# Top-2 dispatch on one core: the first store moved behind the first loads, both groups' first stores issued later

## The chip, the core and the metric

The kernel runs on one core of a Trainium2 chip. The metric is the device time of one execution in microseconds (us); of several executions the median is given. The profile comes from one further execution, taken by the hardware profiler; its times are counted from the start of its span.

## What is computed

For each of 16 x 1024 = 16384 tokens there are 512 float32 values `x` and 8 router logits. The softmax over the logits, the two highest probabilities and their renormalising give two weights per token; the output holds, for each token, its `x` row times the lower weight and its `x` row times the higher one:

```python
topk_probs = topk_probs / np.sum(topk_probs, axis=-1, keepdims=True)
x_expanded = x[:, :, np.newaxis, :].repeat(k, axis=2)
return (x_expanded * topk_probs[..., np.newaxis]).astype(np.float32)
```

The softmax's own sum falls out in the renormalising, so the two weights are the sigmoid of the difference of the two highest logits, with either sign. 33.6 MB of `x` and 0.5 MB of logits are read and 67.1 MB of output are written; each output row is one product.

## The kernel before, in words

**Tiling.** The 16384 tokens lie on 128 partitions with 128 tokens ("rows" below) each. They are worked on in two groups of 65 and 63 rows per partition (`GROUPS`, L42). One input row is 2 KB per partition, one output row, both products, 4 KB. The tile `xs` (L95) holds one group's input rows; the tile `osp` (L96) has room for 18 output rows. Output rows go either to `osp` or back into `xs`, over input rows that are no longer needed (L111 to 115).

**Loads.** A group's input comes in three loads (`LOADS`, L44): 6, 28 and 31 rows in the first group, 4, 28 and 31 in the second. They are issued on SyncE's queue (SP, L139), but the second group's first load goes out on ScalarE's (ACT) queue, behind a small copy (L128) that waits until the first group's fourth store has landed. Behind the first load come the two loads of the logits (L144, L145), for both groups at once.

**Weights.** `top2_weights` (L14 to 38) finds the two highest logits of each token on VectorE (DVE) with max and min, in room borrowed from `osp`, and gets both weights on ACT by two sigmoids, into `WA`.

**Products and stores.** `STORES` (L47 to 50) lists each store as (first row, rows, tile, place): in the first group 3, 15, 16, 15 and 16 rows, alternately from `osp` and `xs`, the first two both from `osp`; in the second 16, 16, 15 and 16. For each entry DVE multiplies the rows by their weights in one instruction (L164) or in two (`cuts`, L152): where `osp` is used again, the first `FREE[g]` rows go ahead, since their place comes free earlier. Of the second group's first entry the last `ACT_ROWS` = 4 rows are multiplied by ACT instead, two instructions a row (L157). Behind the products the entry's store is issued (L176): on SP, but the very first one, of three rows, on ACT.

**Order.** `keep_in_program_order` keeps the loads and stores of a queue in the order of the text. An engine that issues a DMA waits first for what the DMA needs: a store for its products, a load of the second group for the stores that read the rows it overwrites. On the DMA engines the packets of one queue go out in order; a packet of these transfers is one partition's whole contiguous piece, up to 64 KB. So SP's order in the first group is: load 6, logits twice, load 28, load 31, store 15, store 16, store 15, store 16, then the second group's loads of 28 and 31 and its four stores.

Of the kernel before, what the change touches and what calls it, by code (L numbers as in the profile page):

```python
# [1 line left out]

# [4 lines left out]

F32 = mybir.dt.float32
ALU = mybir.AluOpType
ACTF = mybir.ActivationFunctionType  # L10
P = 128


def top2_weights(nc, WA, dlt, room, logits, E):  # L14

    tt = nc.vector.tensor_tensor
    hi, lo, n = None, None, E  # L20
    while n > 1:
        n //= 2
        if hi is None:
            a, b = logits[:, :, 0:n], logits[:, :, n : 2 * n]
            nhi, nlo = room(n), b
            tt(nhi, a, b, op=ALU.max)  # L26
            tt(nlo, a, b, op=ALU.min)  # L27
        else:
            a, b = hi[:, :, 0:n], hi[:, :, n : 2 * n]
            nhi, nlo, tmp = room(n), room(n), room(n)  # L30
            tt(tmp, lo[:, :, 0:n], lo[:, :, n : 2 * n], op=ALU.max)  # L31
            tt(nlo, a, b, op=ALU.min)  # L32
            tt(nlo, nlo, tmp, op=ALU.max)  # L33
            tt(nhi, a, b, op=ALU.max)  # L34
        hi, lo = nhi, nlo
    tt(dlt, hi[:, :, 0], lo[:, :, 0], op=ALU.subtract)  # L36
    nc.scalar.activation(WA[:, :, 0], dlt, ACTF.Sigmoid, scale=-1.0)  # L37
    nc.scalar.activation(WA[:, :, 1], dlt, ACTF.Sigmoid, scale=1.0)  # L38

GROUPS = [65, 63]  # L42

LOADS = [[6, 28, 31], [4, 28, 31]]  # L44
BASE = [0, 1]

STORES = [  # L47
    [(0, 3, "osp", 0), (3, 15, "osp", 3), (18, 16, "xs", 0), (34, 15, "osp", 0), (49, 16, "xs", 33)],
    [(0, 16, "osp", 2), (16, 16, "xs", 0), (32, 15, "osp", 0), (47, 16, "xs", 32)],
]  # L50

L = 18

FREE = [3, 2]

ACT_ROWS = 4


@with_exitstack
def kernel(  # L60
    ctx: ExitStack,
    tc: tile.TileContext,
    x: bass.AP,
    router_logits: bass.AP,
    k: bass.AP,
    out: bass.AP,
):
    nc = tc.nc
    B, S, D = x.shape
    E = router_logits.shape[-1]  # L70
    N = B * S
    assert int(k) == 2 and E == 8 and N == P * sum(GROUPS)
    M = N // P

    x_v, o_v, rl_v = [], [], []
    t0 = 0
    for n in GROUPS:
        t1 = t0 + P * n
        x_v.append(
            x.rearrange("b s d -> (b s) d")[t0:t1].rearrange("(p m) d -> p m d", p=P)  # L80
        )
        o_v.append(
            out.rearrange("b s k d -> (b s) k d")[t0:t1].rearrange(
                "(p m) k d -> p m k d", p=P
            )
        )
        rl_v.append(
            router_logits.rearrange("b s e -> (b s) e")[t0:t1].rearrange(
                "(p m) e -> p m e", p=P
            )  # L90
        )
        t0 = t1

    wpool = ctx.enter_context(tc.tile_pool(name="wpool", bufs=1))
    xs = wpool.tile([P, max(GROUPS), D], F32)  # L95
    osp = wpool.tile([P, L, 2, D], F32)  # L96
    WA = wpool.tile([P, M, 2], F32)
    dlt = wpool.tile([P, M], F32)


    flat = osp.rearrange("p l k d -> p (l k d)")
    taken = [0]

    def room(n):
        o = taken[0]
        taken[0] += M * n
        return flat[:, o : o + M * n].rearrange("p (m n) -> p m n", n=n)

    logits = room(E)

    def place(where, at, n):  # L111

        if where == "osp":
            return osp[:, at : at + n]
        return xs[:, at : at + 2 * n, :].rearrange("p (r k) d -> p r k d", k=2)

    m0 = 0
    stores = []
    for g, G in enumerate(GROUPS):
        x0, r = BASE[g], 0  # L120
        for n in LOADS[g]:

            late = g == 1 and r == 0
            if late:


                rows = xs[:, x0 : x0 + 2, :]
                pause = nc.scalar.activation(rows, rows, ACTF.Copy)  # L128
                tc.add_manual_dep(
                    pause.ins,  # L130
                    stores[-2].ins.name,
                    mybir.DependencyInfo(
                        mybir.DependencyClass.Sync, mybir.DependencyReason.DATA
                    ),
                    reason="begin when the store ahead of the last has landed",
                )
                tc.keep_in_program_order(pause)
            queue = nc.scalar if late else nc.sync
            load = queue.dma_start(xs[:, x0 + r : x0 + r + n, :], x_v[g][:, r : r + n, :])  # L139
            tc.keep_in_program_order(load)  # L140
            r += n
            if g == 0 and r == 6:
                n0 = GROUPS[0]
                tc.keep_in_program_order(nc.sync.dma_start(logits[:, :n0], rl_v[0]))  # L144
                tc.keep_in_program_order(nc.sync.dma_start(logits[:, n0:], rl_v[1]))  # L145
                top2_weights(nc, WA, dlt, room, logits, E)
        assert r == G
        for r, n, where, at in STORES[g]:
            og = place(where, at, n)

            again = where == "osp" and at == 0 and r > 0
            cuts = [0, FREE[g], n] if again else [0, n]  # L152
            if g == 1 and r == 0:
                cuts = [0, n - ACT_ROWS]
                for j in range(n - ACT_ROWS, n):
                    for k2 in range(2):
                        nc.scalar.activation(  # L157
                            og[:, j, k2, :],
                            xs[:, x0 + r + j, :],
                            ACTF.Copy,  # L160
                            scale=WA[:, m0 + r + j, k2 : k2 + 1],
                        )
            for a, b in zip(cuts, cuts[1:]):
                nc.vector.tensor_tensor(  # L164
                    og[:, a:b],
                    xs[:, x0 + r + a : x0 + r + b, :]
                    .unsqueeze(2)
                    .to_broadcast([P, b - a, 2, D]),
                    WA[:, m0 + r + a : m0 + r + b, :]
                    .unsqueeze(3)  # L170
                    .to_broadcast([P, b - a, 2, D]),
                    op=ALU.mult,
                )

            queue = nc.scalar if g == r == 0 else nc.sync
            stores.append(queue.dma_start(o_v[g][:, r : r + n], og))  # L176
            tc.keep_in_program_order(stores[-1])
        m0 += G


# [1 line left out]
_INS = ['x', 'router_logits', 'k']  # L182
_OUTS = [((16, 1024, 2, 512), 'float32')]

_NUMBERS = {'k': 2}


# [26 lines left out]
```

## Time and profile before

| | |
|---|---|
| median of 3 runs | 240.56 us (239.94 to 240.78) |
| span of the profiled execution | 238.1 us |
| DVE, ACT busy in it | 137.6 us, 7.9 us |
| read, written | 34.08 MB, 67.11 MB |
| mean rate over the span | 425 GB/s |
| DMA packets | 2448 |

Of the profiled execution the span alone is known, from its first instruction to its last; the launch and what closes the execution lie outside it. The median of the runs, which are taken without the profiler, is 2.5 us above this span. Busy time of an engine is the time in which it carries out instructions; issuing a DMA and waiting do not count. The DMA engines, sixteen of them, have a row of their own in the 40 slices and shares by queue: q1 is the queue that SP issues to, q10 the one of ACT.

### The profile page before, as it was taken

To read this page: it belongs to the slowest core of one execution; us is meant where nothing else is said; L and a number is where in the kernel's file an instruction comes from. 1 tells how busy PE (TensorE), PEld (TensorE's weight loads), DVE (VectorE), ACT (ScalarE), POOL (GpSimd) and SP (SyncE) were. 2 spreads that over 40 slices of the span, in tenths; PEclk is the share of its full clock that TensorE was granted. 3 is DMA by queue.
4 is the path that set the end of the run, shared out by engine and by line. 5 is a ranking of instruction groups with operands and counts; after the bars stand their busy time and mean duration, and the time that the engine had idled before them with its cause. 6 is when DMAs were issued, how large, how long until landed. Compare 5 with 4: busy or idle time off the path is not lost.

```text
span 238.1 us, 115 instructions
## 1 busy us (share of the span) xinstructions
DVE 137.6 (58%) x22; ACT 7.9 (3%) x12; POOL 0.2 (0%) x4
## 2 busy tenths in 40 slices
DVE  0560499999789999100000009999936999950000
ACT  2000000000000000010000007000000000000000
POOL 0000000000000000000000000000000000000000
DMA  7979998979998999989999899898989989979894
GB/s 262 533 337 519 430 418 374 496 341 495 462 396 374 506 433 392 495 352 483 486 396 417 376 479 501 352 506 363 517 363 451 429 363 495 485 341 517 352 528 176
DMA packets 2448, 101.19 MB, mean 425 GB/s; under 512 B 272, under 2 KB 400, under 8 KB 528
## 3 DMA queue, kind: packets, MB, share of 16 engines
q1 hardware_dynamic: 2160, 98.57, 96.1%
q10 hardware_dynamic: 288, 2.62, 2.6%
HBM read 34.08 MB, written 67.11 MB: 425 GB/s over the span
## 4 chain that ended last, share of the span: by engine, by line
DMA 50%; DVE 38%; SPq 1%; issue 0%; DVEq 0%
DMA xs<-in_x_dram 30%; DVE osp L164 24%; DMA out_dram<-osp 20%; DVE xs L164 14%; SPq L144 0%; SPq L145 0%; SPq L139 0%; SPq L176 0%; DVEq L164 0%
## 5 line engine op out<-in xcount | busy, mean ns | idle before, releaser
L164 DVE TENSOR_TENSOR osp<-xs,WA 128x3072 f32<-128x3072 f32 (+4 forms) x7 | 65.1, 9298 | 65.6 <-DMA xs<-in_x_dram 56.8
L164 DVE TENSOR_TENSOR xs<-xs,WA 128x16384 f32<-128x16384 f32 x4 | 68.9, 17225 | 0.2
L157 ACT ACTIVATE osp<-xs,WA 128x512 f32<-128x512 f32 x8 | 5.0, 708 | 37.6 <-DMA xs<-in_x_dram 37.6
L26 DVE TENSOR_TENSOR osp<-osp 128x512 f32<-128x512 f32 x1 | 0.7, 692 | 8.4 <-DMA osp<-in_router_logits_dram 8.4
L128 ACT ACTIVATE xs<-xs 128x1024 f32<-128x1024 f32 x1 | 1.1, 1056 | 90.8 <-DMA out_dram<-osp 90.8
L37 ACT ACT_TABLE_LOAD x1 | 1.3, 1283 | 0.7 <-PEq L195 0.7
L27 DVE TENSOR_TENSOR osp<-osp 128x512 f32<-128x512 f32 x1 | 0.7, 691 | 0.0
L32 DVE TENSOR_TENSOR osp<-osp 128x256 f32<-128x256 f32 (+1 forms) x2 | 0.7, 350 | 0.0
L31 DVE TENSOR_TENSOR osp<-osp 128x256 f32<-128x256 f32 (+1 forms) x2 | 0.7, 350 | 0.0
L33 DVE TENSOR_TENSOR osp<-osp 128x256 f32<-128x256 f32 (+1 forms) x2 | 0.7, 350 | 0.0
L34 DVE TENSOR_TENSOR osp<-osp 128x256 f32<-128x256 f32 (+1 forms) x2 | 0.7, 348 | 0.0
L37 ACT ACTIVATE WA<-dlt 128x128 f32<-128x128 f32 x1 | 0.3, 317 | 10.3 <-DVE dlt L36 10.3
L36 DVE TENSOR_TENSOR dlt<-osp 128x128 f32<-128x128 f32 x1 | 0.3, 292 | 0.0
L38 ACT ACTIVATE WA<-dlt 128x128 f32<-128x128 f32 x1 | 0.3, 299 | 0.0
L195 POOL MEMSET const-bfloat16-1.0<- 128x1 bf16 x1 | 0.1, 102 | 0.0
L195 POOL MEMSET const-uint8-127<- 128x1 uint8 x1 | 0.1, 102 | 0.0
L195 POOL MEMSET const-float32-1.0<- 128x1 f32 x1 | 0.1, 99 | 0.0
L195 POOL MEMSET const-float32-0.0<- 128x1 f32 x1 | 0.1, 98 | 0.2 <-issue 0.2
## 6 DMA issues: line engine op xcount, KB each, us to landing
out_dram<-osp SPq DMA_DIRECT2D x3, 7680.0 KB, 23.4
xs<-in_x_dram SPq DMA_DIRECT2D x2, 7936.0 KB, 40.9
xs<-in_x_dram SPq DMA_DIRECT2D x2, 7168.0 KB, 35.2
xs<-in_x_dram SPq DMA_DIRECT2D x1, 1536.0 KB, 6.2
out_dram<-osp ACTq DMA_DIRECT2D x1, 1536.0 KB, 24.7
xs<-in_x_dram ACTq DMA_DIRECT2D x1, 1024.0 KB, 24.8
osp<-in_router_logits_dram SPq DMA_DIRECT2D x1, 260.0 KB, 6.4
osp<-in_router_logits_dram SPq DMA_DIRECT2D x1, 252.0 KB, 6.6
```

Of the source, the lines that this page charges most:

```text
L26: tt(nhi, a, b, op=ALU.max)
L27: tt(nlo, a, b, op=ALU.min)
L31: tt(tmp, lo[:, :, 0:n], lo[:, :, n : 2 * n], op=ALU.max)
L32: tt(nlo, a, b, op=ALU.min)
L33: tt(nlo, nlo, tmp, op=ALU.max)
L34: tt(nhi, a, b, op=ALU.max)
L36: tt(dlt, hi[:, :, 0], lo[:, :, 0], op=ALU.subtract)
L37: nc.scalar.activation(WA[:, :, 0], dlt, ACTF.Sigmoid, scale=-1.0)
L128: pause = nc.scalar.activation(rows, rows, ACTF.Copy)
L157: nc.scalar.activation(og[:, j, k2, :], xs[:, x0 + r + j, :], ACTF.Copy, scale=WA[:, m0 + r + j, k2 : k2 + 1],)
L164: nc.vector.tensor_tensor(og[:, a:b], xs[:, x0 + r + a : x0 + r + b, :] .unsqueeze(2) .to_broadcast([P, b - a, 2, D]), WA[:, m0 + r + a : ...
L195: nc = _bacc.Bacc("TRN2", target_bir_lowering=False, num_devices=1)
```

## The change

Three things change, all around the first stores of the two groups.

- The first group's first entry (3 rows) no longer gets its store at once on ACT's queue. It is held, and issued on SP directly ahead of the second entry's store (15 rows), with an added dependency on the last product of that second entry, so that both stores are issued together.
- The product of that second entry is cut into one row and fourteen (`cuts = [0, 1, n]`). The one row is of the first load of six; the fourteen are of the load of 28.
- `ACT_ROWS` goes from 4 to 2: of the second group's first entry, DVE multiplies 14 rows instead of 12, and ACT 2 instead of 4. The store of that entry is one store of 16 rows as before.

On the engines' own lists this is: SP has one store more, DVE one instruction more, ACT a DMA and four activations fewer. Bytes and number of DMAs are the same.

```diff
-ACT_ROWS = 4
+ACT_ROWS = 2
...
-    stores = []
+    stores, held = [], []
...
+            if g == 0 and r == 3:
+                cuts = [0, 1, n]
...
-                nc.vector.tensor_tensor(
+                product = nc.vector.tensor_tensor(
...
-            queue = nc.scalar if g == r == 0 else nc.sync
-            stores.append(queue.dma_start(o_v[g][:, r : r + n], og))
-            tc.keep_in_program_order(stores[-1])
+            held.append((r, n, og))
+            if g == r == 0:
+                continue
+            for r2, n2, og2 in held:
+                stores.append(nc.sync.dma_start(o_v[g][:, r2 : r2 + n2], og2))
+                if r2 < r:
+                    tc.add_manual_dep(
+                        stores[-1].ins,
+                        product.ins.name,
+                        mybir.DependencyInfo(
+                            mybir.DependencyClass.Sync, mybir.DependencyReason.DATA
+                        ),
+                        reason="begin with the store behind it",
+                    )
+                tc.keep_in_program_order(stores[-1])
+            held = []
```

## The prediction

> **What bounds the kernel now.** I read the page first: how much of the span do the DMA engines carry packets, and on which queue?
>
> ```profile
> span 238.1 us, 115 instructions
> ...
> DVE 137.6 (58%) x22; ACT 7.9 (3%) x12; POOL 0.2 (0%) x4
> ...
> DMA  7979998979998999989999899898989989979894
> ...
> q1 hardware_dynamic: 2160, 98.57, 96.1%
> q10 hardware_dynamic: 288, 2.62, 2.6%
> ```
>
> The two queues' packets take 96.1 + 2.6 = 98.7% of sixteen engines' span: 0.987 x 238.1 = 235.0 us. DVE, the busiest engine, has 58%. So the chain of waits has to be read with care:
>
> ```profile
> 2.11 24.91 DMA xs<-in_x_dram
> ...
> 27.04 16.17 DVE osp L164
> ...
> 43.23 22.90 DMA out_dram<-osp
> ...
> 66.15 12.97 DVE osp L164
> ```
>
> It puts 38% of the span on DVE, but while DVE multiplies from 27.04 to 43.21 the DMA engines are moving other rows. A DVE step costs time only where the DMA queue runs empty. The busy time by stretches tells whether it ever does. Its last two columns are the DMA share (packet time of the packets that start in the stretch, so it can pass 1) and GB/s; their quotient is the speed while a packet runs.
>
> ```profile
> core 0: us, DVE busy (x) ACT busy (x) POOL busy (x), PEclk, DMA share, GB/s
> 1.60:1.70 0.10, 0.00 (x0) 0.10 (x1) 0.00 (x0) 1.00 0.00 0
> 1.70:5.90 4.20, 0.00 (x0) 0.31 (x1) 0.00 (x0) 1.00 1.01 366
> 17.70:20.50 2.80, 0.00 (x0) 0.00 (x0) 0.00 (x0) 1.00 0.96 394
> 20.50:23.10 2.60, 0.00 (x0) 0.00 (x0) 0.00 (x0) 1.00 1.00 429
> 23.10:26.40 3.30, 0.00 (x0) 0.00 (x0) 0.00 (x0) 1.00 1.01 386
> 26.40:38.50 12.10, 11.46 (x1) 0.00 (x0) 0.00 (x0) 1.00 1.13 489
> 44.80:47.10 2.30, 2.30 (x1) 0.00 (x0) 0.00 (x0) 1.00 1.02 442
> 47.10:157.50 110.40, 61.85 (x6) 6.07 (x9) 0.00 (x0) 1.00 1.00 435
> 157.50:160.00 2.50, 2.50 (x1) 0.00 (x0) 0.00 (x0) 1.00 1.00 406
> 160.00:216.90 56.90, 46.09 (x4) 0.00 (x0) 0.00 (x0) 1.00 1.00 433
> 236.00:238.00 2.00, 0.00 (x0) 0.00 (x0) 0.00 (x0) 1.00 0.00 0
> ```
>
> The first packet starts between 1.60 and 1.80, none starts after 236.0, and the share is 1.00 over the 110.4 us and the 56.9 us between. There is **no idle DMA time to win**. The speed is 434 GB/s in both long stretches, through loads, stores and the change from one to the other. It is lower in three places: the start (366/1.01 = 362), which the change leaves as it is, 17.7 to 26.4, and 157.5 to 160.0 (406). So a change that moves the same bytes can gain only slow packets, and can lose by letting the queue run empty. I looked for both.
>
> **What the slow packets cost.** At 434 GB/s the bytes of the three rows from 17.7 to 26.4 would need 394 x 2.8/434 = 2.54, 429 x 2.6/434 = 2.57 and 386 x 3.3/434 = 2.94 us; their packets took 0.96 x 2.8 = 2.69, 2.60 and 3.33. Lost: 0.15 + 0.03 + 0.40 = 0.58 us; with the rounding of share and rate, 0.5 to 0.65. From 157.5 to 160.0: 2.50 less 406 x 2.5/434 = 2.34, so 0.16 us. From 44.8 to 47.1: 1.02 x 2.3 less 442 x 2.3/434, which is nothing.
>
> What happens there stands in the timeline:
>
> ```profile
> 12.84 3.36 DVE L164 TENSOR_TENSOR osp<-xs,WA 128x3072 f32<-128x3072 f32 x1 [0.58 <-ACT WA L38]
> 16.23 0.38 ACTq L176 DMA_DIRECT2D out_dram<-osp  x1
> 27.04 16.16 DVE L164 TENSOR_TENSOR osp<-xs,WA 128x15360 f32<-128x15360 f32 x1 [10.85 <-DMA xs<-in_x_dram]
> 43.23 0.35 SPq L176 DMA_DIRECT2D out_dram<-osp  x1
> ...
> 60.48 0.34 SPq L176 DMA_DIRECT2D out_dram<-xs  x1
> ...
> 142.37 12.96 DVE L164 TENSOR_TENSOR osp<-xs,WA 128x12288 f32<-128x12288 f32 x1 [46.00 <-DMA xs<-in_x_dram]
> 155.40 0.34 SPq L176 DMA_DIRECT2D out_dram<-osp  x1
> ...
> 172.67 0.34 SPq L176 DMA_DIRECT2D out_dram<-xs  x1
> ```
>
> The early store is issued on ACT's queue at 16.23, and the packets of the 28-row load that start from 17.7 on are slow until 26.4, when that load's packets are out. The store's packets go on beside the next load from 26.4 to 38.5 at 489/1.13 = 433, at full speed. So taking turns costs nothing in itself; the store's first 10 us beside a load do. The 157.5 place also lies about 2 us behind a store's issue (155.40), before the last load's end.
>
> **The change part by part.** *The three-row store leaves ACT's queue for SP's.* Its cost is its packets' time wherever they stand, so it moves and saves nothing by itself. For how long the packets take, and how many stood ahead of the load's end (queue rows of three windows: 16 to 41, 16 to 23.2, 16 to 20.1):
>
> ```profile
> q10 hardware_dynamic: 144, 1.57, 14.8%
> ```
> ```profile
> q10 hardware_dynamic: 31, 0.38, 12.4%
> ```
> ```profile
> q1 hardware_dynamic: 22, 1.26, 74.4%
> ```
>
> All of it is 0.148 x 25 = 3.7 us on each engine, 0.46 for each of an engine's eight packets; 31 packets, two for each of 16 engines, started before the load's last packet. Without them and without the slow packets the 28-row load lands at 27.02 - 0.92 - 0.58 = 25.5, and both loads are through, where the queue now goes over to the store, at 47.1 - 3.7 - 0.6 = 42.8.
>
> *DVE's product of fifteen rows is cut to one and fourteen.* The durations:
>
> ```profile
> L164 DVE TENSOR_TENSOR osp<-xs,WA 128x12288 f32<-128x12288 f32 x2 | 25.9, 12957 | 48.4 <-DMA xs<-in_x_dram 46.0 <-DMA out_dram<-osp 2.4
> L164 DVE TENSOR_TENSOR osp<-xs,WA 128x15360 f32<-128x15360 f32 x1 | 16.2, 16158 | 10.8 <-DMA xs<-in_x_dram 10.8
> ...
> L157 ACT ACTIVATE osp<-xs,WA 128x512 f32<-128x512 f32 x8 | 5.0, 708 | 37.6 <-DMA xs<-in_x_dram 37.6
> ```
>
> A row is (16.158 - 12.957)/3 = 1.07 us, so fourteen take 15.09. The one row belongs to the first six loaded and runs at 16.2, under the 10.85 us in which DVE waited; without that cover it would put 1.1 us on the store's issue. Fourteen rows from 25.5 end at **40.6**. Both stores are issued then, 0.4 us apart by the 0.35 that one takes, while the loads run to 42.8: **2.2 us ahead**, where today 43.23 stands 3.9 ahead of 47.1. The second store is covered by the 3.7 us of the first.
>
> *What stands behind them.* DVE's next product (17.2 us by 43.23 to 60.48) ends at 57.9 instead of 60.4, its store is needed when the two stores are out, 3.7 us and 18.1 us (15 rows' 7.86 MB at 434) after 42.8, at 64.6: more room than now. The three-row product at 57.9 needs the early store landed, by then some 10 us past. From 66.15 on the queue holds the same bytes in the same order, all 0.6 us earlier. SP waited for DVE there anyway, so nothing is queued behind the added wait, and ACT's next instruction waits for the fourth store, as before.
>
> *Second group: two rows go from ACT to DVE.* ACT loses 4 x 0.708 = 2.8 us, beside idle time. DVE's twelve rows become fourteen, 12.96 to 15.09: from 141.8 to 156.9, against a change of queue at 160.2 - 0.6 = 159.6, **2.7 us ahead** (now 4.8). The next store is ready at 156.9 + 17.2 = 174.1 and needed 19.3 us (the 16 rows' 8.39 MB at 434) after 159.6, at 178.9. Hidden.
>
> **How late may a store be issued?** That decides whether 2.2 and 2.7 us are enough, and no row shows it for a queue about to run dry. Bounds:
>
> ```profile
> 0.73 0.38 SPq L139 DMA_DIRECT2D xs<-in_x_dram  x1
> ```
>
> On idle DMA engines: issued at 0.73, first packet from 1.70: 1.0 us. From above: the early store, issued at 16.23, had no packet until 20.1 (the third queue row above has q1 alone), 3.9 us, but two load packets' turns lie in that. At 1.0 us there is no gap. At 3.9 the gaps are 1.7 and 1.2, 2.9 us. I take the 1.0: in the case at hand the queue has nothing left to take a turn, which is like the idle row. The Trainium skill, "DMA: Bandwidth & Descriptors", section "Latency and other measured facts", gives about 600 ns to the first byte for a queue of SP or ACT; by that estimate too both stores come in time, so it leaves the sum as it is.
>
> *New slow packets* beside the later issue: 0 by the 44.8 row, 0.16 us by the 157.5 row. For the first group I take its own row, 0; for the second the 0.16 stays. **Sum: -0.58 us**, out of 238.1. The 240.56 us median of the runs (239.94 to 240.78) lies 2.5 above the profiled span; I keep that difference. 240.56 - 0.58 = **240.0**.
>
> **The rivals.** *A, forecast:* the slow packets were the early store's and go, 240.0 (-0.24%). For it: they begin 1.5 us behind its issue. Against: 26.4 to 38.5 mixes the same two kinds at full speed. *B, more goes:* the 157.5 row's 0.16 too, since that store now comes as the last load packets already run: -0.74, 239.8, faster by a little over 0.3%. Against: only one of the two such places is slow now. *C, the change doesn't do what it is for:* the load would be slow there with or without a store, and the time stays at 240.56. For it: no row shows the load without the store at that point. *D, the queue runs dry:* a store needs more than 2.2 us from issue to first packet; at 3.9 us, 2.9 us of gaps less 0.58, 242.9. Decided at 2.2 us in the first group, 2.7 in the second; what speaks against it is the 1.0 us row and that today's changes at 3.9 and 4.8 leave a share of 1.00. One queue for loads and stores is what makes the gap possible: today ACT's queue has packets of its own to fill in. The Trainium skill, "Perfetto Trace Analysis", section "DMA Optimizations", advises one issuing engine for inputs and another for outputs; the change goes the other way in the first group, and by that rule D is the case; the trace so far does not bear it out, as both queues share the full 98.7%.
>
> **How the numbers follow.** A measurement of this kernel tells some 0.3%, 0.7 us, from no change: 239.84 is the line. A 0.48, B 0.20, C 0.19, D 0.13. A lies 0.16 from the line, so about 0.12 of its 0.48 may be read as faster; with 0.14 of B that is 0.26 faster. D and nothing else is slower, 0.13. The rest, 0.61, is within. The range has A, B, C with the runs' scatter of 0.4 either way, and the small end of D: 239.4 to 241.0.
>
> **What would show it.** Right: the stretch from 17.7 to the load's end at 434 GB/s; the 28-row load landing near 25.5; both first stores issued at 40.6 to 41.0; a share of 1.00 across 42.8 and 159.6; a span of 237.5. Wrong: no packet starting for a microsecond or more near 42.8 or 159.6 (D); 25 to 27 us for the landing although no store runs (C); DVE's fourteen rows over 15.1 us; a landing later than 25.5 by more than the 2.2 us of room.

## The result and the profile after

The changed kernel takes 241.22 us (median of 22 executions, 239.55 to 241.61), the kernel before beside it 239.93 (22 executions, 239.71 to 241.05): a ratio of 1.0040, 95% interval 1.0028 to 1.0052 (the two medians alone give 1.0054). It is **slower by 0.4%**. The forecast was 240.0, faster by 0.24%.

The times lie in two groups: 4 of the 22 executions at 239.55 to 240.02, 18 at 240.67 to 241.61. Of the kernel before, 18 of 22 lie at 239.7 to 240.2 and 4 above 240.5. The profiled execution of the changed kernel is one of the four, called quick below (239.83 us, 1.8 above its span). From its page:

```profile
span 238.0 us, 111 instructions
...
q1 hardware_dynamic: 2304, 100.14, 97.7%
q10 hardware_dynamic: 144, 1.05, 1.0%
```

The early store has gone from q10 to q1; the two queues together still take 98.7%, and the span is 0.1 us shorter. From the timeline of the same execution:

```profile
25.03 15.09 DVE L166 TENSOR_TENSOR osp<-xs,WA 128x14336 f32<-128x14336 f32 x1 [7.90 <-DMA xs<-in_x_dram]
40.15 0.82 SPq L181 DMA_DIRECT2D out_dram<-osp  x2
...
57.41 0.33 SPq L181 DMA_DIRECT2D out_dram<-xs  x1
...
157.68 0.34 SPq L181 DMA_DIRECT2D out_dram<-osp  x1
```

DVE's fourteen rows take 15.09 us, as worked out; the load landed at 25.0 and the stores were issued at 40.15, half a microsecond ahead of the forecast. Below is the busy time by stretches, with DMA share and GB/s last:

```profile
17.70:26.40 8.70, 1.37 (x1) 0.00 (x0) 0.00 (x0) 1.00 1.00 433
40.40:43.00 2.60, 2.60 (x1) 0.00 (x0) 0.00 (x0) 1.00 1.14 391
104.00:127.00 23.00, 0.00 (x0) 0.78 (x1) 0.00 (x0) 1.00 1.01 437
157.50:160.50 3.00, 2.91 (x2) 0.00 (x0) 0.00 (x0) 1.00 1.44 623
234.80:237.50 2.70, 0.00 (x0) 0.00 (x0) 0.00 (x0) 1.00 0.00 0
```

"Lost" below is worked out as in the prediction: share times length, less the bytes at 434 GB/s. From 17.7 to 26.4 nothing is lost any more. But from 40.4 to 43.0, where the load's last packets run, 1.14 x 2.6 = 2.96 us went into bytes worth 391 x 2.6/434 = 2.34: **0.62 us lost**, where the same packets of the kernel before lost nothing (the prediction's 44.80 row). At 157.5 it is 0 instead of 0.16. So this quick execution gained the 0.58 and paid about as much at another place.

That does not yet explain the other 18 of 22. A second profile of the same kernel (first experiment, 241.60 us, span 239.8) is one of them:

```profile
17.70:26.40 8.70, 1.29 (x1) 0.00 (x0) 0.00 (x0) 1.00 1.00 433
40.40:43.00 2.60, 2.60 (x1) 0.00 (x0) 0.00 (x0) 1.00 1.06 391
104.00:127.00 23.00, 0.00 (x0) 0.76 (x1) 0.00 (x0) 1.00 1.01 431
157.50:160.50 3.00, 2.91 (x2) 0.00 (x0) 0.00 (x0) 1.00 1.36 579
234.80:237.50 2.70, 0.00 (x0) 0.00 (x0) 0.00 (x0) 1.00 0.11 49
```

Lost are 0.41 us at 40.4 to 43.0, 0.4 from 104 to 127 (shares are rounded to 0.01, so 0.1 either way there) and 0.08 at 157.5. The last row is the one to see. The DMA queues' part of the answer for that stretch, and its packet count:

```profile
DMA packets 16, 0.13 MB, mean 49 GB/s; under 512 B 14, under 2 KB 14, under 8 KB 14
...
q1 hardware_dynamic: 16, 0.13, 11.5%
```

In the quick execution no packet of data starts after 234.8. Here two do, of 64 KB each: 14 of the sixteen engines are done but for their closing small packets, and **two engines are still a packet short of the end**. All sixteen together lost little more than in the quick execution, 0.9 us for 0.7; but the kernel ends with the last engine, and the span is 1.8 us longer.

### The profile page after: what moved, and what is told of

Its sections match the earlier page's. It is cut to its first block, busy times and chain, and to the rows that moved or that the text cites. A ratio compares the mean times of both kernels' runs of the same rounds, so it can differ in the third digit from the quotient of the medians.

```text
span 238.0 us, 111 instructions
## 1 busy us (share of the span) xinstructions
DVE 139.9 (59%) x23; ACT 5.4 (2%) x8; POOL 0.2 (0%) x4
## 4 chain that ended last, share of the span: by engine, by line
DMA 49%; DVE 39%; SPq 1%; issue 0%; DVEq 0%
DMA xs<-in_x_dram 29%; DVE osp L166 24%; DMA out_dram<-osp 20%; DVE xs L166 14%; SPq L181 0%; SPq L144 0%; SPq L145 0%; SPq L139 0%; DVEq L166 0%
## 5 line engine op out<-in xcount | busy, mean ns | idle before, releaser
L166 DVE TENSOR_TENSOR osp<-xs,WA 128x3072 f32<-128x3072 f32 (+5 forms) x8 | 67.3, 8423 | 63.5 <-DMA xs<-in_x_dram 54.0
L159 ACT ACTIVATE osp<-xs,WA 128x512 f32<-128x512 f32 x4 | 2.6, 710 | 37.6 <-DMA xs<-in_x_dram 37.6
```

Source lines behind the costliest of these rows:

```text
L159: nc.scalar.activation(og[:, j, k2, :], xs[:, x0 + r + j, :], ACTF.Copy, scale=WA[:, m0 + r + j, k2 : k2 + 1],)
L166: product = nc.vector.tensor_tensor(og[:, a:b], xs[:, x0 + r + a : x0 + r + b, :] .unsqueeze(2) .to_broadcast([P, b - a, 2, D]), WA[:, m0 ...
```

## The experiments

Each was timed beside the kernel before, whose median was 239.8 to 240.0 us throughout. "The first handover" is the change from the last load of the first group to the first big store, near 43 us (47 us in the kernel before); the times in the text are medians.

**The changed kernel once more** (no edit)

> The changed kernel once more, unedited, for the spread of its times and a second profile. Theory H (handover of the first group: the two stores issued together 2.2 us ahead of the loads' end slow or starve the last load packets by an amount that differs from execution to execution): 241.2 again for most executions, and where the profile is of such an execution it shows 1 us or more lost between 40 and 45 us. Theory G (the second group's later store): the loss stands near 157 to 162 instead. If the profile is of one of the few quick executions (span about 238.0), it shows only some 0.6 us lost near 40.5 to 43.

241.50 us, five executions at 241.31 to 241.69, ratio 1.0067 (1.0055 to 1.0079). The profile is the second one above: 0.41 us lost at the first handover, and two late engines at the end. H expected 1 us or more between 40 and 45; it is less there.

**ACT_ROWS = 2 alone, twice**

```diff
-ACT_ROWS = 4
+ACT_ROWS = 2
```

> The kernel before with ACT_ROWS = 2 alone: the second group's first store comes 2.1 us later, the first group is as before. H: no change, 239.9 to 240.0. G: most of the 1.0 us that the whole change costs, 240.9 or more.

> The kernel before with ACT_ROWS = 2 alone, once more. If the 0.16 us lost at the second group's handover goes, as in the first profile of this kernel: 239.65 beside 239.85 for the kernel before, a ratio of 0.999, and no packet slow near 157.5 to 160 us. If the first result was chance: 1.000.

239.64 and 239.65 us, ratios 0.9989 (0.9971 to 1.0007) and 0.9975 (0.9951 to 1.0000). In the first of the two profiles:

```profile
44.60:45.40 0.80, 0.80 (x1) 0.00 (x0) 0.00 (x0) 1.00 3.12 1270
157.50:160.50 3.00, 2.93 (x1) 0.00 (x0) 0.00 (x0) 1.00 1.54 666
```

1.54 x 3 less 666 x 3/434 is 0.02: the 0.16 us of the kernel before has gone at 157.5. But the first group's last sixteen load packets, the first row, lost 3.12 x 0.8 less 1270 x 0.8/434, 0.15 us, in a group that this edit leaves as it was; in the kernel before the same stretch reads

```profile
44.60:45.40 0.80, 0.80 (x1) 0.00 (x0) 0.00 (x0) 1.00 2.94 1270
```

which is 0.01. So a handover's loss differs from one execution to the next by as much as the 0.16 us in question. The second group's later store does not harm; theory G falls. It is at best a gain of 0.1% to 0.25%, which these runs don't clearly separate from none.

**The first group's stores alone** (the changed kernel with ACT_ROWS = 4)

```diff
-ACT_ROWS = 2
+ACT_ROWS = 4
```

> The changed kernel with ACT_ROWS back at 4: only the first group's stores are changed. H: the whole loss stays, about 241.2 in most executions. G: back to 239.9.

242.23 us, 1.0084 (1.0058 to 1.0111): the loss stays, and is larger. The harm is in the first group's part of the change. (In its profile 0.5 us is lost at 157.5 to 160.5 too, and three engines are late.)

**The early store by itself on SP's queue**

```diff
-            held.append((r, n, og))
-            if g == r == 0:
-                continue
...
+            stores.append(nc.sync.dma_start(o_v[g][:, r : r + n], og))
+            tc.keep_in_program_order(stores[-1])
```

> The changed kernel, but the three-row store is issued by itself as soon as its product is done (about 16 us), on SP's queue behind the loads; the fifteen-row store is issued at about 40.5 as in the changed kernel. No store runs beside the first loads, and a store is already queued when they end. H in the form that the queue runs short at the handover: back to 239.9 or a few tenths less. If the move off ACT's queue itself costs (packets of two queues no longer take turns), the loss stays: 241.2.

240.22 us, all eleven executions at 240.03 to 240.45, ratio 1.0007 (0.9991 to 1.0024). The move off ACT's queue is not what costs 1.3 us, though it is not free: `ACT_ROWS` = 2 alone, which differs from this kernel in the first group only and was timed beside the same kernel before, took 239.64. The handover reads

```profile
40.40:43.00 2.60, 2.60 (x1) 0.00 (x0) 0.00 (x0) 1.00 1.31 391
```

It loses more, not less: 1.31 x 2.6 less 391 x 2.6/434 is 1.06 us, and with a store queued since 16 us it cannot be an empty queue. No engine is late.

**The stores issued earlier: near 36 and near 38 us** (ACT multiplies the last 4 or 2 of the fourteen rows)

```diff
-                cuts = [0, 1, n]
+                cuts = [0, 1, n - 4]
+                for j in range(n - 4, n):
+                    for k2 in range(2):
+                        part = nc.scalar.activation(
+                            og[:, j, k2, :],
+                            xs[:, x0 + r + j, :],
+                            ACTF.Copy,
+                            scale=WA[:, m0 + r + j, k2 : k2 + 1],
+                        )
```

> The changed kernel with ACT multiplying the last 4 of the fourteen rows, so that both first stores are issued near 36 us, 4.5 us before the last load packets begin. Theory U: the packets are slowed about equally on all engines, as where a store is queued from 16 us on: one lump of about 1 us, no late engine, 240.2 in nearly all executions. If two stores issued together are what costs: 241.3 as in the changed kernel.

> The changed kernel with ACT multiplying the last 2 of the fourteen rows, so that both first stores are issued near 38 us, about 2.5 us before the last load packets begin. If the rule is that a store which waits in the queue when a load's last packet begins slows that packet on all engines alike, and only a store that comes just then or later leaves the engines uneven: 1 us lost near 41, no late engine, 240.2. If being issued within some 5 us of the loads' end is enough: 241.3.

240.23 us (eleven executions at 240.12 to 240.53) and 240.19 (eleven at 240.11 to 240.28), ratios 1.0019 (1.0010 to 1.0028) and 1.0012 (1.0004 to 1.0021): still a little slower than the kernel before. The second one's issue and stretches:

```profile
38.01 0.82 SPq L189 DMA_DIRECT2D out_dram<-osp  x2
```
```profile
40.40:43.00 2.60, 2.60 (x1) 0.00 (x0) 0.00 (x0) 1.00 1.35 391
104.00:127.00 23.00, 0.00 (x0) 1.06 (x1) 0.00 (x0) 1.00 0.93 404
```

1.17 us lost at the handover, nothing from 104 to 127 (0.93 x 23 = 21.4 us for bytes worth 21.4), and no late engine. The stores are issued two microseconds earlier than in the changed kernel, and none of these 22 executions lies above 240.53.

**The stores issued later: near 41 us** (the fifteen rows uncut)

```diff
-                cuts = [0, 1, n]
+                cuts = [0, n]
```

> The changed kernel without the cut of the fifteen rows into one and fourteen: both first stores come 1.1 us later, near 41.2, 1.7 us before the loads end. Theory U: the last load packets have already begun on all engines, so the delay is as unequal or more, 241.2 to 241.6 in most executions. Theory D of the prediction (queue runs empty): a gap of DMA opens or grows by up to 1.1 us, 242.3.

241.84 us, 1.0079 (1.0065 to 1.0093). Issue and stretches:

```profile
41.07 0.82 SPq L181 DMA_DIRECT2D out_dram<-osp  x2
```
```profile
40.40:43.00 2.60, 2.56 (x2) 0.00 (x0) 0.00 (x0) 1.00 0.95 410
104.00:127.00 23.00, 0.00 (x0) 0.02 (x1) 0.00 (x0) 1.00 1.04 430
```

The time is a little above what U expected (241.2 to 241.6), and the trace is not as U had it: the handover loses **nothing** (2.47 for 2.46), and 1.1 us is lost from 104 to 127 instead. U had the engines brought out of step at the first handover. Against that, for this kernel, also stands the count of the packets that start from 102.0 to 102.7 us:

```profile
DMA packets 32, 1.05 MB, mean 1498 GB/s; under 512 B 16, under 2 KB 16, under 8 KB 16
```

Sixteen of them are large and sixteen small: all engines begin the group's last store within 0.7 us of each other, and some are late at the end all the same (from 234.8 to 237.5 us packets at 121 GB/s still start, which is five of 64 KB; in the quick execution none). D's gap isn't there either: the load's last packets begin at 40.6 to 40.8 and take 2.34 us, and from 42.50 to 43.35 packets of the store start already, at 231 GB/s.

**One row stored early on ACT's queue**

```diff
-    [(0, 3, "osp", 0), (3, 15, "osp", 3), (18, 16, "xs", 0), (34, 15, "osp", 0), (49, 16, "xs", 33)],
+    [(0, 1, "osp", 0), (1, 2, "osp", 1), (3, 15, "osp", 3), (18, 16, "xs", 0), (34, 15, "osp", 0), (49, 16, "xs", 33)],
...
+            if g == r == 0:
+                stores.append(nc.scalar.dma_start(o_v[g][:, r : r + n], og))
+                tc.keep_in_program_order(stores[-1])
+                continue
             held.append((r, n, og))
-            if g == r == 0:
+            if g == 0 and r == 1:
                 continue
```

> The changed kernel, but one of the three early rows is stored by itself on ACT's queue at about 15 us, beside the first loads; the other two go out with the fifteen. Theory F (whichever store is the first of all delays the load packets it begins beside by about 0.6 us, wherever it stands): load packets slow near 18 to 25 us as in the kernel before, none or under 0.2 us lost near 40 to 43, engines in step, no late engine, 239.6 to 239.9. If the loss belongs to the change of direction at the end of a load instead, 0.5 us or more stays at 40 to 43 and 241 in most executions.

240.15 us, eleven at 240.10 to 240.34, which lies between F's 239.6 to 239.9 and the 241 of the other reading. The trace decides:

```profile
17.70:26.40 8.70, 0.73 (x1) 0.00 (x0) 0.00 (x0) 1.00 1.09 469
40.40:43.00 2.60, 2.57 (x2) 0.00 (x0) 0.00 (x0) 1.00 1.25 391
```

F falls: beside the one-row store under 0.1 us is lost, and 1.25 x 2.6 less 391 x 2.6/434 is 0.91 us at the handover. (The big store is issued at 40.78 here, but the load's last sixteen packets begin at 41.8 to 42.2 instead of 40.4 to 41.1, so that the store again comes ahead of them, by 1.0 us.)

**The second group's first load on SP's queue**, in the changed kernel, in the kernel before with ACT_ROWS = 2, and in the uncut one

```diff
-            late = g == 1 and r == 0
+            late = False
```

> The changed kernel with the second group's first load (4 rows) on SP's queue, directly ahead of the 28-row load, and without the small copy on ACT that held it back: no load shares the DMA engines with the fourth and fifth stores from 104 to 127 us any more. Theory U (the stores issued just as the last load packets begin slow these by unequal amounts, 0.0 to 0.8 us from engine to engine; the engines then run out of step, and where the ACT queue's load lies beside the last store of the group one engine falls behind by another 1 to 2 us, which ends the kernel): the first part stays, the second goes, 239.6 to 240.0 with nearly all executions within 0.3 us. Theory Q (the handover itself costs the whole 1.5 us in most executions): 241.3 stays.

> The kernel before with ACT_ROWS = 2 and with the second group's first load on SP's queue, without the copy that held it back (the two edits whose other halves were run alone). If the ACT queue's load beside the stores only does harm where engines are already out of step: as with ACT_ROWS = 2 alone, 239.6 to 239.7. If it always costs: 239.3 or less. If sharing is what keeps the engines in step there: 240 or more, with a late engine from 122 us on.

> The changed kernel with the fifteen rows uncut (stores issued near 41.2, no time lost at the first handover in the earlier run) and the second group's first load on SP's queue without the copy. If the ACT queue's load is what makes engines fall behind: 239.3 to 239.6, the 0.6 us of the first store saved at last. If stores issued that late leave the engines in a worse state whatever follows: 240.5 or more.

240.31 us (239.56 to 240.72) in place of 241.2 to 241.5; 239.73 in place of 239.64; 241.38 in place of 241.84. Without that load beside the group's last store (and without the small copy that held it) the changed kernel is some 1 us faster; to move it gains nothing where the early store went out on ACT's queue. But in the uncut kernel the loss stays without it: 1.00 x 23 less 417 x 23/434, 0.9 us, from 104 to 127. So that load is one place where the loss shows, not its cause.

**The moment at which that load joins the stores.** In the changed kernel the copy on ACT is done twice; in the kernel before with ACT_ROWS = 2 it is made shorter (first edit below), doubled (the first added line of the second edit), and doubled with a short one behind it (all of the second edit).

```diff
-                rows = xs[:, x0 : x0 + 2, :]
+                rows = xs[:, x0 : x0 + 1, 0:64]
```

```diff
                 tc.keep_in_program_order(pause)
+                tc.keep_in_program_order(nc.scalar.activation(rows, rows, ACTF.Copy))
+                part = xs[:, x0 : x0 + 1, 0:192]
+                tc.keep_in_program_order(nc.scalar.activation(part, part, ACTF.Copy))
```

> The changed kernel with the copy on ACT done twice, so that the second group's first load is issued near 105.9 instead of 104.8 us. If one engine falls behind because of the moment at which this load joins the stores (its packets from 107.2 on): the late engine goes and the time falls to about 240.0. If it falls behind because of what the first handover left: 241.2 to 241.5 as before.

> The kernel before with ACT_ROWS = 2 and a copy on ACT that is 1/16 as long, so that the second group's first load is issued near 104.0 instead of 104.7 us (the early store stays on ACT's queue). If the moment of this load decides: slow packets from 107 us on and 241 in a good part of the executions. If the first handover decides: 239.6 to 239.7 as with ACT_ROWS = 2 alone.

> The kernel before with ACT_ROWS = 2 and the copy on ACT done twice: the load of the second group is issued near 105.8, its engines' next packets begin 1.8 to 2.2 us later. Theory J (the load can join an engine's packets some 1.6 us after its issue; where the engines' next packet boundaries lie on both sides of that, some engines take it up a packet earlier, run out of step and one ends late): all boundaries lie behind it, all engines take it up together, 239.6 to 239.8, no late engine. If any other moment than the original one harms: 241.

> As rows2_pause2 with a further short copy, so that the load is issued near 106.2 and the engines' next packets begin 1.4 to 1.85 us later, on both sides of 1.6. Theory J: engines out of step, a late engine, 240.8 to 241.4 in a good part of the executions. Without theory J: as rows2_pause2.

The changed kernel isn't helped by the later joining: 241.08 us, one of six executions quick, at 239.76. The other three kernels have the first handover of the kernel before and differ in the copy alone: 240.93 us with the short one (nine of twelve at 240.8 to 241.4), 239.72 with two (ten of twelve at 239.6 to 239.8), 240.95 with two and a short one (ten of twelve at 240.8 to 241.5). A later load is harmless, one 0.6 us later still is not. The load's issue and the queue rows of the packets that start from 104.0 to 112.2 us, first with two copies, then with the third, and behind them the last stretch of the third:

```profile
105.79 0.34 ACTq L140 DMA_DIRECT2D xs<-in_x_dram  x1
```
```profile
q10 hardware_dynamic: 16, 0.13, 3.8%
```
```profile
106.39 0.34 ACTq L142 DMA_DIRECT2D xs<-in_x_dram  x1
```
```profile
q10 hardware_dynamic: 1, 0.01, 0.2%
```
```profile
234.80:237.50 2.70, 0.00 (x0) 0.00 (x0) 0.00 (x0) 1.00 0.06 24
```

With two copies sixteen packets of that load have started by 112.2. With the third **one** has, the others took the load up a packet of the store later; and at the end there is one 64 KB packet behind all others (0.06 x 2.7 x 16 = 2.6 engine-us, one packet's 2.4). With the short copy it is again a single packet that starts ahead of 109.6, and one late engine. Both profiles fit J: one engine takes up the second stream a packet apart from the rest, and one ends about 1.3 us late. (The profile does not name engines; that it is the same one is inferred.)

J does not carry over to the changed kernel. Its profile with two copies is of the quick execution, 239.76 us, and counts from 104.0 to 112.2 us

```profile
q10 hardware_dynamic: 10, 0.08, 2.4%
```

so ten engines took the load up and six a packet later, and no data packet starts after 234.8: no engine was late. In the second profile above, with two late engines, all sixteen of these packets had started by 112.2. A split of the engines thus neither is enough to make one late nor is needed for it.

**The queue run dry on purpose** (uncut, the load on SP's queue, and one row's product done again ahead of the stores)

```diff
-            for a, b in zip(cuts, cuts[1:]):
+            twice = [(0, 1)] if g == 0 and r == 3 else []
+            for a, b in [*zip(cuts, cuts[1:]), *twice]:
```

> As no_cut_load_sp, and one row's product done a second time before both stores may go: they are issued near 42.3, 0.6 us ahead of the loads' end. If a store needs about 1.0 us from issue to its first packet, as on the idle engines at the start: a gap of about 0.4 us near 43 and 0.4 us more than no_cut_load_sp. If it needs less than 0.6: the same time. If it needs 3.9: the gap would have shown as 2 us already with the stores at 41.2, so 3 us here.

240.95 us, ten at 240.80 to 241.41, which is not slower than the 241.38 without the extra product. Issue and two stretches:

```profile
42.53 0.82 SPq L182 DMA_DIRECT2D out_dram<-osp  x2
```
```profile
42.50:43.35 0.85, 0.82 (x2) 0.00 (x0) 0.00 (x0) 1.00 0.01 0
43.35:43.60 0.25, 0.25 (x1) 0.00 (x0) 0.00 (x0) 1.00 1.86 786
```

No packet of the store starts before 43.35, and then sixteen start within 0.25 us (786 GB/s, 0.20 MB, sixteen of its 12 KB packets): the engines had been waiting. A finer cut gives the first one:

```profile
43.35:43.37 0.02, 0.02 (x1) 0.00 (x0) 0.00 (x0) 1.00 0.03 0
43.37:43.39 0.02, 0.02 (x1) 0.00 (x0) 0.00 (x0) 1.00 4.33 1843
234.80:237.50 2.70, 0.00 (x0) 0.00 (x0) 0.00 (x0) 1.00 0.90 388
```

From the issue to the first packet it is 0.84 to 0.86 us. Here is D's gap, at a lead shorter than that. The engines start the store in step, and 0.85 us is lost from 104 to 127 and 0.5 at 157.5 (0.97 x 23 less 405 x 23/434; 0.94 x 3 less 339 x 3/434). The last row holds sixteen data packets (388 GB/s for 2.7 us): in this kernel all engines end late together, not single ones.

**Put together**, by when the first group's big store was issued (losses from one profile each, good to 0.1 us, in the 104 to 127 column to some 0.2; the last column has the median of all executions):

| first big store issued, us | kernel | lost at 40.4 to 43.0 | lost at 104 to 127 | lost at 157.5 to 160.5 | time, us |
|---|---|---|---|---|---|
| 36, 38 | earlier issue | 1.19, 1.17 | 0.1, 0 | 0, 0 | 240.23, 240.19 |
| 40.0, one queued since 16 | early store on SP | 1.06 | 0.1 | 0 | 240.22 |
| 40.78, load's last packets from 41.8 | one row stored early on ACT | 0.91 | 0.2 | 0 | 240.15 |
| 40.15, 40.23 | the change | 0.62, 0.41 | 0.1, 0.4 | 0, 0.1 | 241.22, 241.50 |
| 40.12 | the change, ACT_ROWS 4 | 0.47 | 0.6 | 0.5 | 242.23 |
| 40.12 | the change, two copies on ACT | 0.62 | 0.1 | 0 | 241.08 |
| 40.08 | the change, load on SP | 0.57 | 0.2 | 0 | 240.31 |
| 41.07 | uncut | 0 | 1.1 | 0 | 241.84 |
| 41.31 | uncut, load on SP | 0 | 0.9 | 0.1 | 241.38 |
| 42.53 | dry | 0, and a gap | 0.85 | 0.5 | 240.95 |

Where nothing else is said, the load's last packets begin at 40.4 to 41.1. What is shown: a store that is issued 1.0 us or more ahead of them makes them lose 0.9 to 1.2 us, once, and the later changes between loads and stores cost 0.2 us or less. A store issued less than 1 us ahead makes them lose part of it, one that comes behind their begin nothing. In the profiles of these last two sorts that are not of a quick execution, more is lost at the next changes, and the time is that of the last engine: single engines fall some 1 to 3 us behind, or, in the dry kernel, all of them. The two quick profiles lost 0.62 and hardly anything later. The kernel before paid 0.58 us at 17.7 to 26.4, beside the early store, and its later changes cost 0.16; there the big store was issued at 43.23, 1.6 us ahead of the load's last packets, and these lost nothing.

What stays open: why engines that lost less at the first handover lose time later, and what makes one execution of the same kernel quick and the next 1.5 us longer (4 of 22 executions of the kernel before lie above 240.5 as well, and none of those was profiled). No run shows the cause inside the DMA engines, and what connects the two losses is seen in the kernels of this table, not derived.

## Why the prediction was wrong

*What bounds the kernel:* right. DMA share 98.7% before and after; DVE's times came as worked out and none of them set the end.

*The starting point, 240.56 us:* **mis-sized.** It was the median of three executions, two of them among the few of this kernel above 240.5; over 22 executions it is 239.93, and the execution lasts 1.8 us longer than its span (239.83 for 238.0), not 2.5. From 239.93 the forecast gain of 0.58 would have been 239.35. That the forecast of 240.0 lies near the kernel before is this term's doing; the change itself was forecast 1.9 us too good.

*The slow packets are the early store's and go (-0.58 us):* **half right.** They went, but the gain did not stay: 0.62 us was lost at 40.4 to 43.0 instead, where the first store now follows the loads. Whether it is the same cost that only moved is not shown: a one-row store beside the loads cost under 0.1 us, and the handover behind it lost 0.91 all the same. The weak point stood in the prediction's own reading: mixing from 26.4 to 38.5 cost nothing, so the store's company alone was not the cost. With -0.58 + 0.62 and the 0.16 at 157.5 that did go, the quick execution's 0.1 us gain is accounted for.

*New slow packets: 0 for the first group by the 44.8 row:* **this term failed first, 0.62 us for 0** in the quick execution, 0.41 in the other. That row shows a handover in a kernel whose first store was issued 27 us earlier (16.23, 43.23); it is no neighbour of a first store. It was also one execution's: with ACT_ROWS = 2 alone the same packets lost 0.15.

*"From 66.15 on the queue holds the same bytes in the same order, all 0.6 us earlier":* **the step that made the sign wrong.** It treats sixteen engines as one. The share and the GB/s are means. 18 of 22 executions are 0.7 to 1.7 us above the kernel before; in the profiled execution of that group (241.60 us, first experiment) two engines are late, while the mean hardly moved. What puts single engines back stays open.

*Rival D:* it does not explain the result. The stores issued at 40.15 and even at 41.07 left no gap at the handover, and the lead at which one opens is below 1 us: about 0.85 us from issue to first packet in the dry kernel, near the 1.0 us bound that was taken and far from 3.9. The Trainium skill ("DMA: Bandwidth & Descriptors", section "Latency and other measured facts") gives about 600 ns to the first byte for these queues. The 0.85 us measured here, counted from the start of the issue, is some 0.25 us longer.

*The rule on separate queues:* the Trainium skill ("Perfetto Trace Analysis", section "DMA Optimizations") says that it may make sense to give loads to one issuing engine and stores to another, especially where there are loops or control flow. The change went against it and was slower, but the queue is not the main reason: the changed kernel with the early store issued by itself on SP's queue was 0.07% slower than the kernel before (-0.09 to 0.24%), and with the second group's first load moved to SP as well, the changed kernel got faster, 240.31. Nor does ACT's queue fill in at the first handover of the kernel before, as the prediction had it: the early store's packets are out by 38.5 us, and the handover is at 47.

*Second group, two rows from ACT to DVE:* cost nothing, as forecast; B's 0.16 us at 157.5 did go, though about as much was lost at the first handover of the kernel with this edit alone.

*The chances:* slower had 0.13, all of it for D. No rival had engines that fall out of step, and the range, with 241.0 as its end, left it out. The shortest median of the study is that of the kernel that keeps the first group as it was and takes ACT_ROWS = 2: 239.64 and 239.65, hardly to be told from the kernel before.

## What to carry to other kernels

A share of 1.00 says that the DMA engines are busy on the mean, not that they end together: count the packets that start in the last microseconds, and where single ones stand behind all others, look for the stretch that put their engine back. A cost that sits beside an operation may come up again where the operation goes; move the operation in a small experiment before counting the cost as gone. And when executions fall in two groups, take more than three before fixing the starting point, and profile one of each group before explaining the median.

## What the runs showed of the hardware that was not expected

- The first change from loads to a big store costs up to 1.2 us of DMA time, in the load's last packets, not in the store's: 1.17 us with the store issued 2.4 us ahead of these packets, 0.62 with it issued 0.4 us ahead, 0 with it issued behind their begin. The kernels that lost nothing there lost 0.9 to 1.1 us from 104 to 127.
- The moment at which a second stream joins a running one can matter: issued at 105.79 us the kernel took 239.72, at 106.39 us 240.95, where one engine took it up a packet apart from the other fifteen. A split of ten and six, in another kernel, did no harm (239.76).
- From the issue of a store on an empty queue to its first packet it took about 0.85 us.
